# Swiglu of a hybrid layer: gate and up as seven block products in place of eight, u through memory, down as its own stage with eight sums side by side

## The chip, the core and the metric

The program runs on one core of one Trainium2 chip. The metric is the device time of one execution in microseconds; of the kernel before there are three runs. Everything is float32. The engines are named as the profile names them: PE (TensorE, the matrix products), PEld (its weight loads), DVE (VectorE), ACT (ScalarE), POOL (GpSimd) and SP (SyncE, which here only issues transfers). A tensor product is made three times, as high part by high part, high by low and low by high, of operands that are split into two float32r numbers.

## The reference, cut to what matters

```python
D_MODEL = 1024; SEQ = 2048; D_FF = 2816
def swiglu(h, w_gu, w_down):
    gate, up = jnp.split(h @ w_gu, 2, axis=-1)
    return (jax.nn.silu(gate) * up) @ w_down

def trunk_layer(x, ctx, mod_x, mod_c, lp, update_ctx):
    ...
    x = x + ga1 * branch_merge(px, fx, rwkv_output(yx, qx, lp), lp)
    hx2 = modulate(rmsnorm(x, lp["norm2_g"]), sh2, sc2)
    x = x + ga2 * swiglu(hx2, lp["w_gu"], lp["w_down"])
    ...
# and at the end: rmsnorm(x, final_norm_g)
```

The rest (input projection, a bidirectional scan, a Fourier branch) is computed by parts of the kernel that the change leaves as they are.

## The kernel before, in words

Data lie transposed: 128 channels on the partitions, tokens along the row. The 2048 tokens go in four blocks of 512 (`TB` gives their order 1, 2, 0, 3), and most tiles are 128x512 float32, 256 KB. Weights come as tiles of 128x128; `load_w` (lines 137 to 146) reads one column tile of a weight from memory in chunks of four rows of tiles (`wraw`, 256 KB each, two buffers), ACT copies the chunk into `whi` (L144, rounding to float32r) and DVE subtracts that for `wlo` (L145); `whi` and `wlo` have two buffers each. `mm3` (lines 148 to 153) then issues three products for each row of tiles: whi by high, whi by low, wlo by high (L151, L152, L153). `split` (L156 on ACT, L157 on DVE) does for activations what `load_w` does for weights. The program is written with tile pools; a scheduler sets the order of each engine's instructions at build time, and each engine then works through its own queue in that order, waiting on semaphores. A pool that is opened after another was closed in the same stretch of memory waits for the last user of that stretch.

Of the kernel's stages these matter here, with their times in the profiled execution:

- `gn_block` (lines 715 to 743), 16 blocks of 128 tokens that bring the scan's output into the layout of the next stage. The last three run between 1965 and 2006 us. Its tiles `gny`, `gnb`, `gnv` have six buffers; its result goes to memory (`o_dr`, L743, from POOL).
- `c_merge` (four token blocks, products named `pr`, 96 each) and `c_out` (products `po`, 192 each), in the order merge 0, merge 1, out 0, merge 2, out 1, merge 3, out 2, out 3. `c_merge` reads `o_dr` as `oraw`, and `gf` and `gr` from memory. `c_out` writes its rows `x1` to memory (`x1_dr`), sums squares (`acc`), and makes the row scale `rs` with a product named `rmsps` (L773), a square root on ACT and a reciprocal on DVE (L162). After out 0 the kernel also makes the SwiGLU's input for that token block at once (`h2_block`, L779 to L781, `XH0`).
- The SwiGLU from 2308 us, for two pairs of token blocks. `ff_in` makes the inputs `xh` and `xl` of a pair. For each of four groups of column tiles (6, 6, 5, 5 of 22), the gate product `pgt` and the up product `put` are made for both blocks of the pair with one load of the weight (24 products for each block and each tile), ACT and DVE make `tg = (tanh + 1) * gate * up` (L890, L891, L898), `split` makes `uh` and `ul`, and the group's part of the down product `pd` is added onto `x1f` in SBUF (L908). After the last group come squares, the sum over channels, the scale, the output (`oo`, L922) and its store.

PSUM has eight banks of 128x512: two in the pool `pmm`, six in `pcx`.

## Time and profile before

| what | us |
|---|---|
| runs: median of three (lowest, highest) | 3793.66 (3787.59, 3802.95) |
| the profiled execution: its span, first to last instruction | 3793.2 |
| PE busy, share of the span | 3527.7, 93% |
| DVE busy, share of the span | 2086.9, 55% |
| ACT busy, share of the span | 1397.3, 37% |
| mean clock granted to PE, of full speed | 0.954 |
| first `pr` product, first `po` product | 1980.1, 2044.1 |
| first `pgt` product, last `pd` product starts | 2308.4, 3767.8 |

The trace gives no time for the profiled execution other than its span, 0.5 us below the median of the runs. The page cuts the span into 40 slices of 95 us; the SwiGLU is the last 15 or so of them. In a row of a group, "busy" is the sum over its instructions, the number behind it the mean of one, and the last column is the time for which the engine stood idle just before them, with what ended it. Times of a product are latencies: products overlap, so their rate is read from counts over a window.

### The profile page before, as it was taken

How to read it: one execution, taken by the hardware profiler on the slowest of the kernel's cores; microseconds unless marked ns; L12 is line 12 of the kernel's file. 1: busy time of each engine (PE TensorE's matmuls, PEld its weight loads, DVE VectorE, ACT ScalarE, POOL GpSimd, SP SyncE). 2: the span in 40 equal slices, each digit the busy share in tenths (PEclk: the TensorE clock that was granted, in tenths of full speed). 3: DMA queues.
4: the chain of work that ended last, by engine and by line, in shares of the span. 5: the costliest groups of instructions: out<-in, count | busy, mean ns of one | idle time of the engine just before them, and what ended most of it. 6: DMA issues, size and time to landing. Idle time of an engine off the chain costs nothing.

```text
span 3793.2 us, 53448 instructions
## 1 busy us (share of the span) xinstructions
PE 3527.7 (93%) x20076; PEld 2885.6 (76%) x20076; DVE 2086.9 (55%) x4157; ACT 1397.3 (37%) x2618; POOL 490.4 (13%) x918
## 2 busy tenths in 40 slices
PE   5979899999999999998989798999999999999997
PEld 4858677677878878787777676888888878888886
DVE  7778776565676666667766664322233552232325
ACT  3776666533343444344443332212111321111122
POOL 0252333311121212121210000000000000000000
PEclk7989899999999999998989899999999999999999
DMA  6456544654454545557766554111111241111112
GB/s 221 138 188 200 165 157 171 212 164 124 139 164 137 154 137 166 166 147 234 214 205 227 167 192 144 46 55 42 53 44 53 88 141 44 54 46 49 50 49 69
DMA packets 282323, 494.75 MB, mean 130 GB/s; under 512 B 86576, under 2 KB 106032, under 8 KB 281552
## 3 DMA queue, kind: packets, MB, share of 16 engines
q1 hardware_dynamic: 241280, 363.74, 31.2%
q0 software_dynamic: 40784, 127.59, 10.1%
q8 instruction: 158, 2.59, 0.3%
q14 instruction: 101, 0.83, 0.1%
HBM read 371.00 MB, written 120.21 MB: 129 GB/s over the span
## 4 chain that ended last, share of the span: by engine, by line
PE 42%; issue 7%; DMA 2%; DVE 1%; ACT 1%; POOL 1%; SPq 0%; DVEq 0%; POOLq 0%; ACTq 0%
PE pd L152 4%; PE pd L153 4%; PE pd L151 4%; PE pgt L152 4%; PE pgt L151 4%; PE pgt L153 4%; PE put L153 4%; PE put L152 4%; PE put L151 4%; DMA gnb<-y_dr 1%; PE pf L152 0%; PE pf L151 0%; DMA gr<-g_dr 0%; PE pf L153 0%; POOL x_dr L822 0%
## 5 line engine op out<-in xcount | busy, mean ns | idle before, releaser
L144 ACT ACTIVATE whi<-wraw 128x512 fp32r<-128x512 f32 (+2 forms) x682 | 383.7, 600 | 1130.1 <-PE pd L152 338.7
L145 DVE TENSOR_TENSOR wlo<-wraw,whi 128x512 fp32r<-128x512 f32 (+2 forms) x682 | 427.9, 654 | 328.5 <-ACT whi L144 324.8
L151 PE MATMUL pgt<-xh,whi 128*128 128x512 f32 x704 | 276.6, 393 | 11.9 <-ACT xh L780 11.8
L151 PE MATMUL put<-xh,whi 128*128 128x512 f32 x704 | 275.3, 391 | 0.0
L152 PE MATMUL put<-xl,whi 128*128 128x512 f32 x704 | 275.0, 391 | 0.0
L153 PE MATMUL put<-xh,wlo 128*128 128x512 f32 x704 | 274.8, 390 | 0.0
L152 PE MATMUL pgt<-xl,whi 128*128 128x512 f32 x704 | 274.7, 390 | 0.1
L153 PE MATMUL pgt<-xh,wlo 128*128 128x512 f32 x704 | 274.6, 390 | 0.0
L152 PE MATMUL pd<-ul,whi 128*128 128x512 f32 x704 | 273.7, 389 | 0.0
L153 PE MATMUL pd<-uh,wlo 128*128 128x512 f32 x704 | 273.5, 389 | 0.0
L151 PE MATMUL pd<-uh,whi 128*128 128x512 f32 x704 | 273.2, 389 | 0.0
L151 PE MATMUL pxps<-hh,whi 128*128 128x512 f32 (+2 forms) x720 | 256.4, 357 | 17.6 <-ACT hh L198 6.3
L151 PE MATMUL fps<-fhh,whi 128*128 128x512 f32 x640 | 267.9, 419 | 3.8 <-ACT fhh L416 3.0
L152 PE MATMUL fps<-fhl,whi 128*128 128x512 f32 x640 | 259.7, 406 | 4.1 <-DVE fhl L417 4.1
L152 PE MATMUL pxps<-hl,whi 128*128 128x512 f32 (+2 forms) x720 | 254.5, 354 | 7.1 <-DVE hl L199 7.1
L153 PE MATMUL fps<-fhh,wlo 128*128 128x512 f32 x640 | 259.2, 405 | 0.0
L153 PE MATMUL pxps<-hh,wlo 128*128 128x512 f32 (+2 forms) x720 | 250.7, 350 | 0.2 <-DVE wlo L145 0.2
L908 DVE SCALAR_TENSOR_TENSOR x1f<-pd,ga2h,x1f 128x512 f32<-128x512 f32 x128 | 96.1, 751 | 279.1 <-PE pd L153 279.1
L898 DVE TENSOR_TENSOR tg<-tg,put 128x512 f32<-128x512 f32 x88 | 60.4, 687 | 261.0 <-PE put L153 260.9
L522 DVE TENSOR_TENSOR tm<-Q,AI 128x126 f32<-128x126 f32 (+22 forms) x558 | 141.1, 253 | 59.1 <-DMA AI<-ab_dr 34.6
L151 PEld LDWEIGHTS pxps<-hh,whi 128*128 128x128 f32 x720 | 141.6, 197 | 41.2 <-ACT hh L198 7.9
L151 PEld LDWEIGHTS pgt<-xh,whi 128*128 128x128 f32 x704 | 132.8, 189 | 41.5 <-ACT xh L780 13.0
(391 smaller groups left out, 7367.2 us busy)
## 6 DMA issues: line engine op xcount, KB each, us to landing
wraw<-w_in SPq DMA_DIRECT2D x250, 256.0 KB, 3.4
wraw<-w_gu SPq DMA_DIRECT2D x176, 256.0 KB, 3.0
ld<-zt_dr SPq DMA_DIRECT2D x36, 768.0 KB, 4.7
ld<-qr_dr SPq DMA_DIRECT2D x36, 512.0 KB, 6.3
wada<-w_ada SPq DMA_DIRECT2D x32, 512.0 KB, 4.6
g_dr<-fo POOLq DMA_DIRECT2D x64, 256.0 KB, 4.0
wraw<-w_out SPq DMA_DIRECT2D x64, 256.0 KB, 3.1
wraw<-w_down SPq DMA_DIRECT2D x64, 256.0 KB, 2.7
```

Source lines behind the costliest of these rows:

```text
L144: nc.scalar.activation(out=hi[:, k0:k1, :], in_=raw, func=AF.Copy)
L145: nc.vector.tensor_tensor(out=lo[:, k0:k1, :], in0=raw, in1=hi[:, k0:k1, :].bitcast(F32), op=ALU.subtract)
L151: nc.tensor.matmul(ps, wh[:, k, :], xh(k), start=start and k == 0, stop=False)
L152: nc.tensor.matmul(ps, wh[:, k, :], xl(k), start=False, stop=False)
L153: nc.tensor.matmul(ps, wl[:, k, :], xh(k), start=False, stop=stop and k == K - 1)
L522: nc.vector.tensor_tensor(out=tm[:, 0:M, 0:n], in0=Q[:, 0:M, j:j + 1].to_broadcast([128, M, n]), in1=AI[:, j, j + 1:32].unsqueeze(1).to_br ...
L898: nc.vector.tensor_tensor(out=tg, in0=tg, in1=pu, op=ALU.mult)
L908: nc.vector.scalar_tensor_tensor(out=x1[:, ct, :], in0=pd, scalar=ga2h[:, ct:ct + 1], in1=x1[:, ct, :], op0=ALU.mult, op1=ALU.add)
```

## The change

Gate and up for one column tile f of both and for both token blocks of a pair are seen as one product of 2x2 blocks: rows gate and up, inner halves (channels 0 to 511 and 512 to 1023, four tiles each), columns the two token blocks. It is made with seven block products (`B11`, `B21`, `T2`, `T3`, `T1`, `T4`, `B22`, twelve matrix products each) in place of eight, with sums of blocks before and after.

- The input side: the class `Operands` makes seven operands for a pair from `x1_dr`, split into high and low (`build(k)` for each of four tile indexes: four scalings on DVE, four biases on ACT, two differences on POOL, two on DVE, seven splits on ACT and DVE). For the first pair this lies inside the last `c_out`; `h2_block` and the pools around it go. For the second pair it lies inside the first `down`, with its reads issued from POOL.
- The weight side, in `up`: four chunks are read straight (`wA`, six buffers with `wS`), four sums or differences are made on DVE (`op`, L928), and seven operands are split into tiles with seven buffers (`hilo`).
- The result side, in `up`: one copy from PSUM on ACT (L956), seven additions on DVE (`add`, L941), two gates (L945 on ACT, L946 on DVE) and two products (L950 on DVE) whose results `u` go to memory (`u_dr`, from POOL). `B11` and `B21` use the two banks of `pmm`, the others the five of `pcx`; the eighth bank (`rm`) is for `rmsps`.
- `B11` and `B21` of the first three column tiles are made early, behind the last `c_out`.
- `down` is a stage of its own for each of the four token blocks: for each of 22 tiles f it reads a row of w_down (two chunks, through `load_w`) and u (one chunk, `ur`), splits them, and issues 24 products into eight sums that stay in eight banks; at the end they are added onto `x1` (L1024), squares and scale follow, and the output is stored (L1033, L1034). w_down is laid out by rows f on the host.
- The order is up of pair 0, down, down, up of pair 1, down, down.
- `c_merge` and `c_out` have the same work; their tiles lie in two pools (`ea` on the right side of SBUF, `eb` on the left, where the pool of `gn_block` was), with one buffer in each for `mh`, `ml` and `x1`, and eight buffers `t2` in `eb` in place of seven on the right side. `rs` of the last block is made inside `up`.

```diff
-    fa = ctx.enter_context(tc.tile_pool(name="fa", bufs=1))
-    pcx = ctx.enter_context(tc.tile_pool(name="pcx", bufs=6, space=PS))
+    u_dr = [D_([128, SEQ], f"u_dr{f}") for f in range(FT)]
...
+    pcx = fst.enter_context(tc.tile_pool(name="pcx", bufs=5, space=PS))
...
-        ps = pcx.tile([128, 512], F32, tag="cx", name="rmsps2")
+        ps = pcx.tile([128, 512], F32, tag="rm", name="rmsps2", bufs=1)
...
+    eb = eps.enter_context(tc.tile_pool(name="eb", bufs=1))
...
+    ea = eas.enter_context(tc.tile_pool(name="ea", bufs=1, side="right"))
...
+    def t2(name):
+        return eb.tile([128, 512], F32, tag="t2", name=name, bufs=8)
...
+    def out_stats(n, acc, rs):
+        sum_rs(acc, rs)
+        nc.gpsimd.dma_start(rs1_dr[TB[n]], rs[0:1, :])
+    OPS = ("B11", "B21", "T2", "T3", "T1", "T4", "B22")
+    class Operands:
+        def __init__(self, blk2, tmp, eng):
+            self.blk2, self.tmp, self.eng = blk2, tmp, eng
+            self.X = {o: [fh.tile([128, 4, 512], F32R, tag=f"{y}{o}", name=f"{y}{o}_{blk2}") for y in "hl"] for o in OPS}
...
+        def build(self, k):
+            b = {}
+            for m in range(2):
+                for hf in range(2):
+                    t0, kk = 512 * TB[2 * self.blk2 + hf], k + 4 * m
+                    x_ = b[m, hf] = self.tmp("x_")
+                    self.eng.dma_start(x_, x1_dr[:, kk, t0:t0 + 512])
+                    nc.vector.scalar_tensor_tensor(out=x_, in0=x_, scalar=gsc2[:, kk:kk + 1], in1=self.rs[hf], op0=ALU.mult, op1=ALU.mult)
+                    nc.scalar.activation(out=x_, in_=x_, func=AF.Identity, bias=mod[:, 24 + kk, 0:1])
+            b11, b12, b21, b22 = b[0, 0], b[0, 1], b[1, 0], b[1, 1]
+            t3 = self.tmp("t3")
+            def put_(o, x):
+                split(self.X[o][0][:, k, :], self.X[o][1][:, k, :], x)
+            def sub(o, x, y, eng=nc.gpsimd):
+                eng.tensor_tensor(out=o, in0=x, in1=y, op=ALU.subtract)
+            put_("B11", b11)
+            put_("B21", b21)
+            sub(t3, b22, b12)
+            sub(b12, b12, b11, nc.vector)
+            sub(b11, b22, b12, nc.vector)
+            put_("T2", b11)
+            put_("T3", t3)
+            put_("T1", b12)
+            sub(b21, b21, b11)
+            put_("T4", b21)
+            put_("B22", b22)
+    M = {}
+    M[0] = c_merge(0)
+    for n in range(3):
+        M[n + 1] = c_merge(n + 1)
+        acc = t2("acc")
+        c_out(n, M[n], acc)
+        out_stats(n, acc, t2("rs"))
+    eas.close()
+    fh = fst.enter_context(tc.tile_pool(name="fh", bufs=1, side="right"))
+    ops0 = Operands(0, t2, nc.sync)
+    acc3 = fh.tile([128, 512], F32, tag="rs", name="acc3", bufs=3)
+    c_out(3, M[3], acc3, lambda ct: ops0.build(ct // 2) if ct % 2 else None)
+    early = {}
+    for f in range(3):
+        w = load_w(I["w_gu"][f], KT)
+        early[f] = {}
+        for m, o in enumerate(OPS[:2]):
+            ps = pcx.tile([128, 512], F32, tag="cx", name="e" + o) if f < 2 else pmm.tile([128, 512], F32, tag="mm", name="e" + o)
+            mm3(ps, [x[:, 4 * m:4 * m + 4, :] for x in w], lambda k: ops0.X[o][0][:, k, :], lambda k: ops0.X[o][1][:, k, :], 4, 512)
+            early[f][o] = ps
+    eps.close()
+    ff = fst.enter_context(tc.tile_pool(name="ff", bufs=1))
+    def tmp(name):
+        return ff.tile([128, 512], F32, tag="t2", name=name, bufs=8)
+    def raw_(name):
+        return ff.tile([128, 512], F32, tag="raw", name=name, bufs=6)
+    def hilo(name):
+        return [ff.tile([128, 4, 128], F32R, tag=f"w{y}", name=f"{name}{y}", bufs=7) for y in "hl"]
+    def up(blk2, X, early, after=None):
+        TT = [512 * TB[2 * blk2 + hf] for hf in range(2)]
+        for f in range(FT):
+            if f == 1 and after:
+                after()
+            u2 = tmp("u2")
+            A = []
+            for src in (I["w_gu"][f], I["w_gu"][FT + f]):
+                for k0 in (0, 4):
+                    r = raw_("wA")
+                    nc.sync.dma_start(r.rearrange("p (k c) -> p k c", c=128), src[:, k0:k0 + 4, :])
+                    A.append(r)
+            a11, a12, a21, a22 = A
...
+            def prod(x, o):
+                if f in early and o in early[f]:
+                    return early[f][o]
+                ps = pmm.tile([128, 512], F32, tag="mm", name="p" + o) if o in OPS[:2] else pcx.tile([128, 512], F32, tag="cx", name="p" + o)
+                w = hilo("w" + o)
+                h_, l_ = [z.rearrange("p k c -> p (k c)") for z in w]
+                split(h_, l_, x)
+                mm3(ps, w, lambda k: X[o][0][:, k, :], lambda k: X[o][1][:, k, :], 4, 512)
+                return ps
...
+            def gate(c):
+                g_ = tmp("tg")
+                nc.scalar.activation(out=g_, in_=c, func=AF.Tanh, scale=0.5)
+                nc.vector.scalar_tensor_tensor(out=g_, in0=g_, scalar=1.0, in1=c, op0=ALU.add, op1=ALU.mult)
+                return g_
+            def u_out(hf, c, g_):
+                nc.vector.tensor_tensor(out=c, in0=c, in1=g_, op=ALU.mult)
+                nc.gpsimd.dma_start(u_dr[f][:, TT[hf]:TT[hf] + 512], c)
+            s1 = raw_("wS")
+            op(s1, a21, a22, ALU.add)
+            p = prod(a11, "B11")
+            nc.scalar.activation(out=u2, in_=p, func=AF.Copy)
+            op(a21, a11, a21, ALU.subtract)
+            op(a11, s1, a11, ALU.subtract)
+            p = prod(a12, "B21")
+            c11 = tmp("c11")
+            add(c11, u2, p)
+            op(a12, a12, a11, ALU.subtract)
+            p = prod(a11, "T2")
+            add(u2, u2, p)
+            g0 = gate(c11)
+            p = prod(a21, "T3")
+            u3 = tmp("u3")
+            add(u3, u2, p)
+            p = prod(s1, "T1")
+            add(u2, u2, p)
+            c22 = tmp("c22")
+            add(c22, u3, p)
+            p = prod(a22, "T4")
+            add(u3, u3, p)
+            u_out(0, u3, g0)
+            p = prod(a12, "B22")
+            add(u2, u2, p)
+            u_out(1, c22, gate(u2))
+    def down(tb, between=None):
+        t0 = 512 * tb
+        def bank(ct):
+            if ct == 7:
+                return pcx.tile([128, 512], F32, tag="rm", name="pd7", bufs=1)
+            return (pcx if ct < 5 else pmm).tile([128, 512], F32, tag="cx" if ct < 5 else "mm", name=f"pd{ct}")
+        PD = [bank(ct) for ct in range(7)]
+        OPN = {}
+        def load(f):
+            w = load_w(I["w_down"][f], KT)
+            r = ff.tile([128, 512], F32, tag="ur", name="u_", bufs=2)
+            nc.sync.dma_start(r, u_dr[f][:, t0:t0 + 512])
+            u = hilo("u")
+            h_, l_ = [z.rearrange("p k c -> p (k c)") for z in u]
+            split(h_, l_, r)
+            return w, h_, l_
+        def mm(f, ct):
+            (wh, wl), uh, ul = OPN[f]
+            for i, (x, y) in enumerate(((wh, uh), (wh, ul), (wl, uh))):
+                nc.tensor.matmul(PD[ct], x[:, ct, :], y, start=f == 0 and i == 0, stop=f == FT - 1 and i == 2)
+        for f in range(2):
+            OPN[f] = load(f)
+            for ct in range(7):
+                mm(f, ct)
+        PD.append(bank(7))
+        for f in range(2):
+            mm(f, 7)
+        for f in range(2, FT):
+            OPN[f] = load(f)
+            for ct in range(8):
+                mm(f, ct)
+            if between:
+                between(f)
+        X1 = []
+        acc = fh.tile([128, 512], F32, tag="rs", name=f"accf{tb}", bufs=3)
+        for ct in range(8):
+            x1 = tmp("x1f")
+            X1.append(x1)
+            nc.sync.dma_start(x1, x1_dr[:, ct, t0:t0 + 512])
+            nc.vector.scalar_tensor_tensor(out=x1, in0=PD[ct], scalar=ga2h[:, ct:ct + 1], in1=x1, op0=ALU.mult, op1=ALU.add)
...
+    up(0, ops0.X, early, lambda: out_stats(3, acc3, fh.tile([128, 512], F32, tag="rs", name="rs3", bufs=3)))
+    ops1 = Operands(1, raw_, nc.gpsimd)
+    down(TB[0], lambda f: ops1.build(f // 4 - 1) if f % 4 == 0 and 4 <= f < 20 else None)
+    down(TB[1])
+    up(1, ops1.X, {})
+    down(TB[2])
+    down(TB[3])
...
-        "w_gu": tiles(a["w_gu"][0]), "w_down": tiles(a["w_down"][0]),
+        "w_gu": tiles(a["w_gu"][0]), "w_down": np.ascontiguousarray(a["w_down"][0].reshape(FT, 128, KT, 128)),
```

Three places show how the instructions move. The first is SP's queue between the last blocks of `gn_block` (L716 to L720) and merge 0. Before:

```order
L718 DMA gnv_18497<-bv_dr_69 128x512
L797 DMA oraw_18587<-o_dr_95 128x512
L797 DMA oraw_18591<-o_dr_95 128x512
L797 DMA oraw_18595<-o_dr_95 128x512
L716 DMA gny_18531<-y_dr0_93 128x512
L797 DMA oraw_18599<-o_dr_95 128x512
L801 DMA gf_18603<-fm_dr0_98 128x512
L803 DMA gr_18605<-g_dr8_80 128x512
L720 DMA sg_18537<-sg_dr_70 128x128
L717 DMA gnb_18532<-y_dr1_94 128x512
```

In the changed kernel, from the same read of `gnv` on (`x1_1` is the row tile of out 0, 2 MB):

```order
L718 DMA gnv_18497<-bv_dr_69 128x512
L819 DMA x1_1_19076<-xT 128x8x512
L716 DMA gny_18531<-y_dr0_93 128x512
L720 DMA sg_18537<-sg_dr_70 128x128
L717 DMA gnb_18532<-y_dr1_94 128x512
L718 DMA gnv_18533<-bv_dr_69 128x512
L800 DMA oraw_18607<-o_dr_95 128x512
L800 DMA oraw_18611<-o_dr_95 128x512
L800 DMA oraw_18615<-o_dr_95 128x512
L800 DMA oraw_18619<-o_dr_95 128x512
```

The reads of merge 0 stood among those of the last `gn_block`; now they stand behind all of them, and the row tile of out 0 stands ahead of the last block's reads.

The second place is DVE's queue in the last `c_out`. Before, one column tile is an addition onto `x`, two `wlo` and an addition of squares, and after the last one `rmsps` and the reciprocal follow, and then the input of the SwiGLU's second block:

```order
L821 SCALAR_TENSOR_TENSOR x_3_20543<-po,ga1h,x_3_20543 128x512
L145 TENSOR_TENSOR wlo<-wraw,whi 128x512 x2
L826 TENSOR_TENSOR acc<-acc,sqk 128x512
L160 TENSOR_SCALAR rs<-rmsps_20865 128x512
L162 RECIPROCAL rs<-rs 128x512
L779 SCALAR_TENSOR_TENSOR a__20879<-x__20880,gsc_263,rs_20877 128x512
L781 SCALAR_TENSOR_TENSOR xl_1_20876<-a__20879,mod,xh_1_20875 128x512
```

In the changed kernel (`hB`, `lB`, `hT`, `lT` are the high and low parts of the operands):

```order
L145 TENSOR_TENSOR wlo<-wraw,whi 128x512 x2
L829 TENSOR_TENSOR acc_20553<-acc_20553,sqk 128x512
L857 SCALAR_TENSOR_TENSOR x__20634<-x__20634,gsc_263,rs_0_0_20549 128x512
L857 SCALAR_TENSOR_TENSOR x__20638<-x__20638,gsc_263,rs_0_1_20551 128x512
L857 SCALAR_TENSOR_TENSOR x__20642<-x__20642,gsc_263,rs_0_0_20549 128x512
L824 SCALAR_TENSOR_TENSOR x_3_20554<-po,ga1h,x_3_20554 128x512
L157 TENSOR_TENSOR lB_0_20536<-x__20634,hB_0_20535 128x512
L857 SCALAR_TENSOR_TENSOR x__20646<-x__20646,gsc_263,rs_0_1_20551 128x512
L157 TENSOR_TENSOR lB_0_20538<-x__20642,hB_0_20537 128x512
```

Between the additions onto `x` there now stand scalings and low parts of the operands. From the first addition of this `c_out` to the last low part, DVE's queue holds 24 scalings or additions onto `x`, 62 other operations on 128x512 and two reciprocals.

The third place is where a pair of token blocks ends and the next begins. Before, on DVE (two blocks finish together; `pgt` and `put` are the next pair's first products):

```order
L160 TENSOR_SCALAR rsf_1_25535<-rmsps_25536 128x512
L922 SCALAR_TENSOR_TENSOR oo<-x1f_0_20927,vec,rsf_0_25505 128x512 x8
L162 RECIPROCAL rsf_1_25535<-rsf_1_25535 128x512
L145 TENSOR_TENSOR wlo<-wraw,whi 128x512
L922 SCALAR_TENSOR_TENSOR oo<-x1f_1_20929,vec,rsf_1_25535 128x512 x8
L891 SCALAR_TENSOR_TENSOR tg<-tg,pgt 128x512 x2
L898 TENSOR_TENSOR tg<-tg,put 128x512 x2
```

In the changed kernel, on DVE, from the second `down` to the second `up` (`c`, `u` are the sums after the products, `pB`, `pT` the products):

```order
L160 TENSOR_SCALAR rsf_26469<-rmsps_26470 128x512
L157 TENSOR_TENSOR wB22l<-wA,wB22h 128x512
L162 RECIPROCAL rsf_26469<-rsf_26469 128x512
L1033 SCALAR_TENSOR_TENSOR x1f<-x1f,vec,rsf_26469 128x512 x8
L941 TENSOR_TENSOR c_26539<-u_26491,pB_26522 128x512
L941 TENSOR_TENSOR u_26491<-u_26491,pT_26542 128x512
L946 SCALAR_TENSOR_TENSOR tg<-tg,c_26539 128x512
```

and on PE at the same place, within the last of the seven products of the first column tile (`pB_26656` is `B11` of the second column tile):

```order
L151 MATMUL pB_26622<-hB_1_24431,wB22h 128x512
L780 MATMUL rmsps_26470<-accf_26422,cn 128x512
L152 MATMUL pB_26622<-lB_1_24432,wB22h 128x512
L153 MATMUL pB_26622<-hB_1_24431,wB22l 128x512
L151 MATMUL pB_26656<-hB_1_24419,wB11h 128x512
```

On PE `rmsps` stands behind 79 products of the new pair, and on DVE the first sum that frees a bank of the new pair stands behind the scale and the eight outputs of the old block.

199 lines of the change are left out of this document (62 added, 137 removed).

## The prediction

> **What bounds the kernel now.** I read the page first: busy times, slices and the chain.
>
> ```profile
> PE 3527.7 (93%) x20076; PEld 2885.6 (76%) x20076; DVE 2086.9 (55%) x4157; ACT 1397.3 (37%) x2618; POOL 490.4 (13%) x918
> PE   5979899999999999998989798999999999999997
> DVE  7778776565676666667766664322233552232325
> PE 42%; issue 7%; DMA 2%; DVE 1%; ACT 1%; POOL 1%; SPq 0%; DVEq 0%; POOLq 0%; ACTq 0%
> ```
>
> PE is the longest, and in the SwiGLU (last 16 slices) it is full but for the last, with DVE at two to five tenths. Next the windows: length, then busy time and count on PE, PEld, DVE, ACT and POOL, then granted clock, DMA share and GB/s.
>
> ```profile
> 2400.00:3000.00 600.00, 600.00 (x2649) 496.99 (x2648) 188.66 (x301) 112.58 (x208) 0.00 (x0) 1.00 0.17 52
> 3000.00:3100.00 100.00, 97.62 (x427) 79.68 (x426) 69.42 (x104) 35.13 (x61) 0.00 (x0) 1.00 0.47 152
> ```
>
> 600 us hold 2649 products at full clock, one per 0.2265 us, with no gap. There only fewer products shorten anything. The second window has the boundary of the pairs, the one stop inside.
>
> **Part 1, the products.** For a pair and a column tile f, gate and up were 2 x 2 x 24 = 96 products; now 7 x 12 = 84. Over 22 tiles and two pairs 528 go: 528 x 0.2265 = **-119.6 us**, if PE stays dense. Whether DVE lets it, these groups tell (busy, mean ns | idle before):
>
> ```profile
> L157 DVE TENSOR_TENSOR ul<-tg,uh 128x512 fp32r<-128x512 f32 x88 | 60.5, 688 | 28.7 <-ACT uh L156 28.6
> L898 DVE TENSOR_TENSOR tg<-tg,put 128x512 f32<-128x512 f32 x88 | 60.4, 687 | 261.0 <-PE put L153 260.9
> L891 DVE SCALAR_TENSOR_TENSOR tg<-tg,pgt 128x512 f32<-128x512 f32 x88 | 60.1, 684 | 156.1 <-ACT tg L890 156.1
> L156 ACT ACTIVATE uh<-tg 128x512 fp32r<-128x512 f32 x88 | 55.0, 625 | 193.3 <-DVE tg L898 193.1
> 2187.97 2.43 DVE L157 TENSOR_TENSOR ol<-oraw,oh 128x512 fp32r<-128x512 f32 x4
> ```
>
> In `up` DVE has 22 operations for each f: 7 low parts, 4 operand sums, 7 additions, 2 gates, 2 products. At 0.687 alone that is 15.1 us, at the 0.61 of the last row (four in 2.43, back to back) 13.4. PE needs 84 x 0.2265 = 19.03. ACT has 10, at 0.625 6.3 us. A weight buffer of `hilo` frees one f before it is needed again, and a bank (seven for seven products) likewise, so a wait up to several us is covered; I take PE as the bound. What could hide here is a gap behind each DVE operation; that is a rival below.
>
> **Part 2, merge 0.** Its reads now wait for `gn_block`'s pool, whose last transfer goes out here:
>
> ```profile
> 1980.00:2044.00 64.00, 54.25 (x216) 41.18 (x217) 47.77 (x81) 25.26 (x48) 2.15 (x3) 0.90 0.89 301
> 2005.85 0.71 POOL L743 DMA_DIRECT2D o_dr<-gnb  x1 [11.88 <-DMA gr<-g_dr]
> gf<-fm_dr SPq DMA_DIRECT2D x32, 256.0 KB, 4.6
> ```
>
> Before, the two merges run from 1980 to 2044 us with DMA 0.89 busy: 192 products need 43.5 of the 64. Now they start about 2006 + 4.6 (a landing) = 2010.6, and dense they end at 2054: +10; if the reads run early there is no loss, if DMA stays the limit behind the late start it is twice that. I take **+9** (0 to +18).
>
> **Part 3, out 0 to merge 2.** `h2_block` goes (16 DVE operations and a reciprocal between out 0 and merge 2). PE's waits at the start of merge 2 and of merge 3, which has no such block ahead:
>
> ```profile
> 2105.55 0.79 PE L151 MATMUL pr<-oh,whi 128*128 128x512 f32 x1 [14.19 <-ACT oh L156]
> 2123.28 0.79 PE L151 MATMUL pr<-oh,whi 128*128 128x512 f32 x1 [4.49 <-ACT whi L144]
> 2186.08 1.22 PE L151 MATMUL pr<-oh,whi 128*128 128x512 f32 x2 [2.81 <-ACT oh L156]
> 2188.65 0.80 PE L152 MATMUL pr<-ol,whi 128*128 128x512 f32 x1 [1.35 <-DVE ol L157]
> ```
>
> Merge 2 becomes like merge 3: 18.68 - 4.16 = **-14.5 us**. The splits of `oraw` then come last, as there.
>
> **Part 4, the last `c_out` and the SwiGLU's start.**
>
> ```profile
> 2260.60:2304.70 44.10, 44.08 (x194) 35.99 (x192) 21.49 (x29) 12.58 (x23) 4.31 (x8) 1.00 0.41 136
> 2304.70:2346.00 41.30, 26.84 (x88) 20.36 (x89) 17.16 (x21) 8.65 (x13) 1.05 (x2) 0.79 0.55 188
> 2322.86 0.80 PE L151 MATMUL pgt<-xh,whi 128*128 128x512 f32 x1 [7.44 <-ACT xh L780]
> 2323.45 0.63 PE L151 MATMUL put<-xh,whi 128*128 128x512 f32 x1
> 2327.62 0.39 PE L152 MATMUL put<-xl,whi 128*128 128x512 f32 x1
> 2327.85 0.39 PE L153 MATMUL put<-xh,wlo 128*128 128x512 f32 x1
> PE rmsps L773 <- DVE acc L826: 2.6, 1, 2.6
> 3771.70 3.35 DVE L162 RECIPROCAL rsf<-rsf 128x512 f32<-128x512 f32 x1 [1.25 <-ACT rsf L161]
> 3784.19 5.39 DVE L922 SCALAR_TENSOR_TENSOR oo<-x1f,vec,rsf 128x512 f32<-128x512 f32 x8
> ```
>
> `c_out` 3 fills 44.1 us, and in the next 41.3 PE makes 88 products, two of them `rmsps`: 85.4 - 86 x 0.2265 = 65.9 us until a dense SwiGLU would have begun. Now the operands of pair 0 are made inside, and DVE's queue holds 24 scalings (0.67, eight in 5.39), 62 others (0.61) and two reciprocals (3.35): 60.6 us, longer than PE's 43.5. The queue's start waits for the first sum, 24 products or 5.4 us: 66; its last part waits for the reads of the last `x1`, a landing and four short operations, about 6.5: 72.5. PE meanwhile makes 72 early products, 16.3 us ahead: 56. DVE gives PE the operands tile by tile, and some early products wait too; for those hand-offs I leave 4. So 60 for 66: **-6** (-13 to +5). POOL's eight differences stand beside this; the nearest row on that engine is a fill of the same size, and above it stands DVE's reciprocal, 0.53 to 3.35 each:
>
> ```profile
> L516 POOL MEMSET Q<- 128x512 f32 x18 | 9.5, 526 | 37.7 <-DMA tb_dr<-Q 37.7
> ```
>
> DVE then has other tiles to work on; uncovered, two in the last tile would cost 1 to 7 us, inside the bound. At out 2 to out 3, `rmsps` (2.6 us wait) goes behind other products: **-2**.
>
> **Part 5, the seams.** `up` and `down` alternate with new sums, so there are five seams where before there was one. The last `pd` product of the kernel, the one seam, and the kernel's end:
>
> ```profile
> 3767.82 0.40 PE L153 MATMUL pd<-uh,wlo 128*128 128x512 f32 x1
> 3048.85 1.13 PE L773 MATMUL rmsps<-acc,cn 128*128 128x512 f32 x2 [2.38 <-DVE acc L913]
> 3768.00:3794.00 26.00, 2.20 (x5) 0.50 (x4) 19.93 (x22) 3.17 (x4) 0.00 (x0) 0.63 0.46 161
> ```
>
> The seam cost 2.4 + 1.1 = 3.5, which goes: **-3.5**. Up to down: all banks but two are free; the last additions, 2 each, two times: **+4**. Down to down: the new block's first products wait for the eight additions onto `x1` (0.7 each, PE needs one bank after the other) and `rmsps` (1.1); and on DVE the reciprocal (3.35) and the outputs (5.4) stand ahead of some `wlo`, where two f of products (10 us) cover: **+6** each (2 to 12), twice, **+12**. Down to up (once): PE has the 79 products of the third order place, 17.9 us, plus `rmsps` 1.1, and then needs a bank that DVE frees behind additions, root (0.6), reciprocal (3.35) and outputs (5.4), at about 8 x 0.7 + 7 x 0.7 + 1.1 + 0.7 + 0.6 + 3.35 + 5.4 + 0.7 = 22 to 30 us from the end of the block, so 5 to 8 us idle. After the idle time of 7.44 the first eleven products took 4.76 us (2322.86 to 2327.62) instead of 2.49, 2.3 us more, and from there they stand 0.23 apart; after the 2.38 the window shows full clock. **+10** (4 to 15). The Trainium skill, "TensorE: Matmul & The Clock Gate", "The HAM clock gate", puts the point at an idle window of about 3.4 us, which both rows agree with; by it the two down-to-down seams would add up to 4.6 if they idle so long. Sum of seams **+26** (14 to 45), and **-3.5**.
>
> **Part 6, `down` itself.** 22 x 24 x 0.2265 = 119.7 us for a block, as many products as before. Per f: 5.44 us of PE, three low parts on DVE (2.1), three copies on ACT (1.9), 768 KB by
>
> ```profile
> wraw<-w_out SPq DMA_DIRECT2D x64, 256.0 KB, 3.1
> wraw<-w_down SPq DMA_DIRECT2D x64, 256.0 KB, 2.7
> ```
>
> or 145 GB/s. The `c_out` window has the same two chunks through the same two buffers for 24 products, at 136 GB/s, and 194 products in 44.1 us, dense. So nothing is added; the 44 writes of `u` from POOL and the operands of pair 1 (four times 13 DVE operations, 9 us in four f, 22 us) lie beside it.
>
> **Part 7, the end.** After the last product 25.1 us remain (3767.8 + 0.4 to 3793.2), with two reciprocals and twice eight outputs. Now one block ends: eight additions and squares (6), `rmsps`, root, reciprocal, eight outputs, a landing: 20: **-5** (-9 to 0).
>
> **The sum.** -119.6 + 9 - 14.5 - 6 - 2 - 3.5 + 26 - 5 = -115.6. The profiled execution's 3793.2 becomes 3677.6; the median of the runs stands 0.5 above its span: **3678**.
>
> **The rivals.** *DVE paces `up`.* 22 operations with seven hand-offs exposed, each as long as an operation (0.69): 15.1 + 4.8 = 20.0 per f, 1 above PE's, x 44 = +43: 3721. For it: a sum waits for ACT and PE in turn. Against: one f of buffers. *Every seam costs as the worst stops here* (14.19 + 4.49 = 18.7): 5 x 18.7 = 94 for 26, with end and start as above, some +84 for hand-offs of operands too: 3762. *`down` starves, slower than before*: a chunk's buffer comes free only behind its low part, two buffers, three chunks. A buffer's round is a landing, a copy (0.63) and a low part (0.69): 4.4 us at 3.1. If landings take 4.6, as `gf`'s, and the low part stands behind two other DVE operations, it is 7.3 per f instead of 5.44: 88 x 1.86 = +164: 3842. It decides from (3793.7 - 3678) / 88 = 1.31 more per f, 6.75 us. Against it stands the dense `c_out`. *DVE empties behind each operation, slower too*: with gaps of half an operation to a whole one (0.34 to 0.69) 22 of them take 22.6 to 30.3 us per f, 3.6 to 11.3 above PE's, x 44 = +158 to +497: 3836 to 4175; it decides from a gap of 0.30. The four operations in 2.43 and eight in 5.39, without such gaps, nearly exclude it. The Trainium skill, "VectorE: DVE Perf Modes", "The DRAIN you can't avoid", states such a gap, of about the duration less 266 ns (0.42, by which the kernel would take 3913). That the products do not fall is excluded by the order, which has them.
>
> **How the numbers follow.** Forecast 0.71 (3646 to 3722, with all unknown costs at their lower ends, -12 - 9 - 7 - 4 = -32, or their upper, 19 + 9 + 11 + 5 = +44); DVE 0.10; seams 0.07; starving in full 0.04, near break-even 0.02; DVE emptying 0.02; better than 3645, by seams that cost nothing, 0.04. The range reaches over the forecast and the DVE case, to 3740: 0.19 is left out. 0.5% (19 us, about what a measurement can tell) bounds the chances: faster 0.71 + 0.10 + 0.07 + 0.04 = 0.92, same 0.02, slower 0.04 + 0.02 = 0.06 (starving near break-even counts as the same).
>
> **What would show it.** Right: in a 400 us window of `up` and of `down` PE full, 4.41 products per us, DVE at 0.7 to 0.8 in `up`; first `po` near 2053; seams of 2 to 10 us; about 20 us behind the last product. Wrong: PE waits for low parts or additions inside `up` (DVE case), for `wraw` copies or `u` inside `down` (starving), seams near 20, or an `up` group on DVE with gaps of 0.3 or more behind each operation.

## The result, and the profile after

The changed kernel takes 3702.55 us (median of four runs, 3702.01 to 3713.41) against 3794.4 for the kernel before (four runs, 3787.59 to 3802.95): a ratio of 0.9766, 95% interval 0.9744 to 0.9787. It is faster by 91.9 us, where 116 were forecast; 3702.55 lies in the range of 3645 to 3740, 24.6 above the forecast value. The profiled execution has a span of 3700.3 us, 92.9 less than before, and the account below is made against that.

From the page of the changed kernel: busy times, the slices of PE and DVE, the chain.

```profile
PE 3424.6 (93%) x19548; PEld 2796.1 (76%) x19548; DVE 2495.4 (67%) x4765; ACT 1595.9 (43%) x2898; POOL 579.3 (16%) x1038
PE   5989889999999999999996999899999999999997
DVE  7777776566676675668776667877785477777344
PE 23%; issue 9%; DVE 2%; DMA 1%; POOL 1%; ACT 0%; SPq 0%; DVEq 0%; POOLq 0%; ACTq 0%
```

PE has the 528 products less (20076 to 19548), DVE 409 us more. DVE is now at 0.7 to 0.8 where `up` runs, and PE's slices are full there all the same. The windows, one in the first `up`, one in the first `down`, one in the last but one:

```profile
2400.00:2700.00 300.00, 300.00 (x1325) 248.43 (x1324) 222.98 (x347) 96.95 (x157) 16.80 (x31) 1.00 0.26 84
2760.00:2860.00 100.00, 100.00 (x443) 82.81 (x442) 53.81 (x82) 43.45 (x76) 9.14 (x8) 1.00 0.54 172
3440.00:3550.00 110.00, 110.00 (x487) 91.12 (x486) 45.07 (x71) 37.70 (x66) 0.00 (x0) 1.00 0.45 147
```

1325 products in 300 us are 4.42 per us, as before. So the two long stages are dense, as forecast, and all of the difference lies between them. PE's waits there, from the timeline (start, duration, what waited, how long and for what):

```profile
2334.82 0.79 PE L151 MATMUL pT<-hT,wT2h 128*128 128x512 f32 x1 [9.56 <-ACT wT2h L156]
2751.36 0.50 PE L1003 MATMUL pd<-uh,whi 128*128 128x512 f32 x1 [1.02 <-ACT whi L144]
2759.11 0.50 PE L1003 MATMUL pd<-uh,whi 128*128 128x512 f32 x1 [2.02 <-ACT whi L144]
2895.34 0.80 PE L1003 MATMUL pd<-uh,whi 128*128 128x512 f32 x1 [6.98 <-ACT whi L144]
3023.65 0.80 PE L151 MATMUL pB<-hB,wB11h 128*128 128x512 f32 x1 [8.72 <-ACT u L956]
3577.74 0.80 PE L1003 MATMUL pd<-uh,whi 128*128 128x512 f32 x1 [6.47 <-ACT whi L144]
3684.14 2.07 PE L780 MATMUL rmsps<-accf,cn 128*128 128x512 f32 x2 [5.74 <-DVE accf L1029]
```

They are the start of the first `up`, the third row of w_down after the first and third `down` (2895, 3577), the second column tile of the second `up` (3023), and the end. Behind each of the long ones a product takes 0.80 in place of 0.39: PE starts again at the slow clock.

For the account by stages the scan's last product (`pz`) is a good mark, since the code ahead of it is the same in both kernels. Before, then after:

```profile
L594 PE MATMUL pz<-UV,BT x1152: 222/222/370, 825.6 to 1971.5; 128*64 128x64 f32 x192
```

```profile
L594 PE MATMUL pz<-UV,BT x1152: 222/222/369, 827.1 to 1963.7; 128*64 128x64 f32 x192
L151 PE MATMUL pr<-oh,whi x128: 387/389/796, 1995.0 to 2205.1; 128*128 128x512 f32 x128
L151 PE MATMUL po<-mh,whi x256: 389/389/397, 2047.6 to 2294.2; 128*128 128x512 f32 x128
```

| stage | before | after | difference | forecast |
|---|---|---|---|---|
| start to the scan's last product | 1971.5 | 1963.7 | -7.8 | 0 |
| to the first `po` | 72.6 | 83.9 | +11.3 | +9 |
| to the start of out 3 (2260.6, 2249.3) | 216.5 | 201.7 | -14.8 | -16.5 |
| to where a dense SwiGLU would begin | 65.9 | 71.0 | +5.1 | -6 |
| the products of the SwiGLU at 0.2265 | 1435.1 | 1315.5 | -119.6 | -119.6 |
| its waits up to the last product | 6.6 | 42.6 | +36.0 | +22.5 |
| the rest to the end | 25.0 | 21.9 | -3.1 | -5 |
| sum | 3793.2 | 3700.3 | -92.9 | -115.6 |

Out 3 starts with the first of the last 192 `po` products. The fourth line is made as in the prediction: from there to 2345 us are 95.7 us with 109 products of the SwiGLU, 95.7 - 24.7. The first line is not counted as the change's: the profiled executions of the experiments, with the same code ahead of that mark, have it between 1957 and 1974 us. So of the 92.9 us some 85 belong to the change in this pair of executions, and 23 to 31 us of the forecast gain (counted with and without that line) did not come: 11 at the first `up`'s start and 13 in the seams, for the most part.

### The profile page after: what moved, and what is told of

Its sections match the earlier page's. It is cut to its first block, busy times and chain, and to the rows that moved or that the text cites. A ratio compares the mean times of both kernels' runs of the same rounds, so it can differ in the third digit from the quotient of the medians.

```text
span 3700.3 us, 54802 instructions
## 1 busy us (share of the span) xinstructions
PE 3424.6 (93%) x19548; PEld 2796.1 (76%) x19548; DVE 2495.4 (67%) x4765; ACT 1595.9 (43%) x2898; POOL 579.3 (16%) x1038
## 3 DMA queue, kind: packets, MB, share of 16 engines
q8 instruction: 155, 2.54, 0.3%
## 5 line engine op out<-in xcount | busy, mean ns | idle before, releaser
L144 ACT ACTIVATE whi<-wraw 128x512 fp32r<-128x512 f32 x560 | 333.2, 626 | 704.3 <-PE pd L1003 196.0
L145 DVE TENSOR_TENSOR wlo<-wraw,whi 128x512 fp32r<-128x512 f32 x560 | 374.4, 688 | 369.7 <-ACT whi L144 356.2
L941 DVE TENSOR_TENSOR u<-u,pT 128x512 f32<-128x512 f32 x176 | 120.8, 686 | 142.6 <-PE pT L153 140.8
L1003 PEld LDWEIGHTS pd<-uh,whi 128*128 128x128 f32 x704 | 133.2, 189 | 53.2 <-ACT whi L144 22.5
L152 PEld LDWEIGHTS pxps<-hl,whi 128*128 128x128 f32 x720 | 142.1, 197 | 29.0 <-DVE hl L199 8.7
L153 PEld LDWEIGHTS pxps<-hh,wlo 128*128 128x128 f32 x720 | 141.6, 197 | 21.3 <-issue 4.8
L1003 PEld LDWEIGHTS pd<-ul,whi 128*128 128x128 f32 x704 | 133.4, 189 | 27.6
L1003 PEld LDWEIGHTS pd<-uh,wlo 128*128 128x128 f32 x704 | 132.1, 188 | 28.7 <-DVE wlo L145 1.4
L152 PEld LDWEIGHTS fps<-fhl,whi 128*128 128x128 f32 x640 | 123.4, 193 | 35.5 <-issue 5.4
L524 DVE TENSOR_TENSOR Q<-Q,tm 128x126 f32<-128x126 f32 (+22 forms) x558 | 140.7, 252 | 13.6
```

The source lines that it names most:

```text
L144: nc.scalar.activation(out=hi[:, k0:k1, :], in_=raw, func=AF.Copy)
L145: nc.vector.tensor_tensor(out=lo[:, k0:k1, :], in0=raw, in1=hi[:, k0:k1, :].bitcast(F32), op=ALU.subtract)
L152: nc.tensor.matmul(ps, wh[:, k, :], xl(k), start=False, stop=False)
L153: nc.tensor.matmul(ps, wl[:, k, :], xh(k), start=False, stop=stop and k == K - 1)
L524: nc.vector.tensor_tensor(out=Q[:, 0:M, j + 1:32], in0=Q[:, 0:M, j + 1:32], in1=tm[:, 0:M, 0:n], op=ALU.subtract)
L941: nc.vector.tensor_tensor(out=o, in0=x, in1=y, op=ALU.add)
```

## The experiments

Each is one edit of the changed kernel unless it says otherwise. Since the stages ahead of the merges vary, time is also counted from the first `po` product to the end: 1652.7 us in the changed kernel (3700.3 - 2047.6). That figure has a spread of its own: e11, which alters nothing behind the first `po`, has 1647.4, so the changed kernel's trace is the slower of the two that can be compared over the whole stretch. Differences under about 5 us are therefore believed only where the waits of the trace show them.

| run | median, us (lowest, highest) | ratio to before, interval | first `po` to end |
|---|---|---|---|
| e1_twelve_more | 3827.35 (3821.73, 3829.66) | 1.0089 (1.0071, 1.0108) | 1774.2 |
| e2_low_twice | 3708.85 (3693.29, 3710.27) | 0.9781 (0.9751, 0.9811) | 1659.3 |
| e3_rs_pool | 3703.86 (3697.29, 3714.55) | 0.9771 (0.9749, 0.9794) | 1649.8 |
| e4_outs_pool | 3711.94 (3707.91, 3714.1) | 0.9789 (0.9774, 0.9804) | 1656.0 |
| e5_own_u2 | 3696.05 (3690.63, 3702.89) | 0.9749 (0.973, 0.9768) | 1645.6 |
| e7_no_early | 3709.92 (3707.51, 3717.22) | 0.9775 (0.9751, 0.9799) | 1663.9 |
| e8_subs_dve | 3692.11 (3684.43, 3696.35) | 0.9746 (0.9715, 0.9777) | 1647.9 |
| e9_x1_late | 3700.0 (3694.69, 3705.76) | 0.9767 (0.974, 0.9794) | 1651.4 |
| e10_all | 3693.14 (3689.81, 3693.85) | 0.9747 (0.9724, 0.977) | 1630.5 |
| e11_merge0_right | 3690.41 (3683.24, 3692.12) | 0.9722 (0.9701, 0.9744) | 1647.4 |
| e12_best | 3669.13 (3663.5, 3679.52) | 0.9673 (0.9647, 0.9699) | 1632.6 |

### Do the products set the pace?

```diff
-            def prod(x, o):
+            def prod(x, o, times=1):
...
-                mm3(ps, w, lambda k: X[o][0][:, k, :], lambda k: X[o][1][:, k, :], 4, 512)
+                for _ in range(times):
+                    mm3(ps, w, lambda k: X[o][0][:, k, :], lambda k: X[o][1][:, k, :], 4, 512)
...
-            p = prod(a12, "B22")
+            p = prod(a12, "B22", 2)
```

> The last block product of every column tile (B22) is made twice, the second time over the first, so that PE has 96 products for a pair and a column tile as before the change; everything else of the changed kernel stays. Products set the pace of up: 528 x 0.2265 = +119.6 us on the changed kernel's 3702.6, 3822. Rival, DVE or the hand-offs set the pace of up: part of the added products lies in waits that are there anyway, under +80, 3780 or less. By the first, 3822 against 3794 before is also the price of all the rest of the change, +28.

Measured from the first `po`: 1774.2 - 1652.7 = +121.5 us. The 528 products cost what the rate says (119.6), within the spread, and no large part of them was hidden. The other half of the answer is the ratio to before, 1.0089: with the products given back, the rest of the change costs 35 us (3827.35 against 3792.17 in the same comparison). The prediction's other terms add up to +4. That is where it was off. The next edit makes the low part of each weight operand twice:

```diff
                 split(h_, l_, x)
+                nc.vector.tensor_tensor(out=l_, in0=x, in1=h_.bitcast(F32), op=ALU.subtract)
```

> In up the low part of each of the seven weight operands is made twice, with the same result, so that DVE has 29 operations for a column tile in place of 22. In the changed kernel's up 347 DVE operations took 222.98 us of 300, 0.643 each. Theory, PE sets the pace and DVE's operations follow each other without gaps: 29 x 0.643 = 18.6 us, just under PE's 19.03, PE stays full, 0 to +6 us. Rival, DVE sets the pace as soon as the sum of its operations with their hand-offs comes near: 29 x 0.687 = 19.9 and more, +39 us or over.

The windows of the first and the second `up` with 29 DVE operations for each column tile:

```profile
2400.00:2700.00 300.00, 300.00 (x1325) 248.41 (x1324) 285.87 (x469) 94.78 (x158) 16.72 (x31) 1.00 0.27 87
3100.00:3400.00 300.00, 300.00 (x1326) 248.39 (x1325) 282.50 (x458) 97.43 (x159) 17.25 (x32) 1.00 0.25 83
```

DVE is 0.95 busy, with 0.61 us per operation (285.87 / 469), and PE still makes 1325 products. The +6.6 us lie at the seams. The wait at 3029, behind the second `up`'s first tile, is 10.40 us, where DVE now has more to work off; the one at 3585 is 8.48, but `down` isn't altered, and other runs have 6.19 to 7.37 there, so that part may be spread. DVE's pace was no near danger: seven more operations for each tile fitted.

### The seams between blocks

What DVE, SP and ACT do ahead of the wait of 6.98 us, and PE and DMA in windows of 5 us around it, in the changed kernel:

```profile
2880.22 5.38 DVE L1033 SCALAR_TENSOR_TENSOR x1f<-x1f,vec,rsf 128x512 f32<-128x512 f32 x8
2885.52 1.28 DVE L145 TENSOR_TENSOR wlo<-wraw,whi 128x512 fp32r<-128x512 f32 x2
2885.57 0.33 SPq L1023 DMA_DIRECT2D x1f<-x_dr  x1
2885.99 0.85 SPq L1034 DMA_DIRECT2D out_T<-x1f  x2
2887.42 1.37 SPq L1034 DMA_DIRECT2D out_T<-x1f  x2
2888.89 0.43 SPq L143 DMA_DIRECT2D wraw<-w_down  x1
2891.43 3.32 SPq L1023 DMA_DIRECT2D x1f<-x_dr  x4
2894.66 0.63 ACT L144 ACTIVATE whi<-wraw 128x512 fp32r<-128x512 f32 x1 [5.63 <-DMA wraw<-w_down]
```

```profile
2875.00:2880.00 5.00, 5.00 (x23) 3.99 (x22) 5.00 (x5) 1.92 (x4) 0.00 (x0) 1.00 0.09 12
2880.00:2885.00 5.00, 4.21 (x19) 3.15 (x18) 5.00 (x9) 1.90 (x3) 0.00 (x0) 1.00 0.92 305
2890.00:2895.00 5.00, 0.00 (x0) 0.00 (x0) 0.00 (x0) 0.34 (x1) 0.00 (x0) 0.66 0.97 331
```

The chunk of w_down goes out at 2888.89, behind stores of the old block (which wait for DVE's outputs) and reads of `x1` for the end of the next block (which wait for the stores' buffers), and ACT can copy it 5.8 us later where the median landing is 2.9, with DMA 0.97 busy. Either could be the cause. There is a third candidate: the chunk goes into one of two buffers, which is free when a low part on DVE (2885.52) has read it, and that low part stands behind the eight outputs. First SP's queue:

```diff
-            nc.sync.dma_start(x1, x1_dr[:, ct, t0:t0 + 512])
+            nc.gpsimd.dma_start(x1, x1_dr[:, ct, t0:t0 + 512])
...
-            nc.sync.dma_start(out_T[128 * k:128 * k + 128, t0:t0 + 512], X1[k])
+            nc.gpsimd.dma_start(out_T[128 * k:128 * k + 128, t0:t0 + 512], X1[k])
```

> The reads of x1 and the stores of the output in down go out from POOL and no longer from SP. Theory, SP's queue: at the end of a block the stores wait for DVE's eight outputs and the reads of the next x1 for the buffers that the stores free, and the chunks of w_down stand behind them; the two waits of 6.98 and 6.47 us go, and the slow clock behind each (2.3), -16 to -18 us, 3685. Rival, DVE's queue (the reciprocal and eight outputs ahead of the low parts): the waits stay at 4 or more each, at most -6, 3697.

```profile
2901.94 0.80 PE L1003 MATMUL pd<-uh,whi 128*128 128x512 f32 x1 [4.02 <-ACT whi L144]
3581.84 0.50 PE L1003 MATMUL pd<-uh,whi 128*128 128x512 f32 x1 [1.54 <-ACT whi L144]
3592.19 0.80 PE L1003 MATMUL pd<-uh,whi 128*128 128x512 f32 x1 [4.60 <-ACT whi L144]
```

6.98 became 4.02, 6.47 became 1.54 + 4.60, and in all nothing was gained (1656.0): a miss. SP is free, but the same 4 MB go out at the same moment, and a later chunk is late. Then the crowd, with the stores left on SP:

```diff
+        X1 = []
...
+            if f == 14:
+                for ct in range(8):
+                    x1 = tmp("x1f")
+                    X1.append(x1)
+                    nc.gpsimd.tensor_copy(x1[:, 0:1], OPN[f][1][:, 0:1].bitcast(F32))
+                    nc.sync.dma_start(x1, x1_dr[:, ct, t0:t0 + 512])
...
-        X1 = []
...
-            x1 = tmp("x1f")
-            X1.append(x1)
-            nc.sync.dma_start(x1, x1_dr[:, ct, t0:t0 + 512])
+            x1 = X1[ct]
```

> The reads of x1 in down are held back until the 15th of the 22 rows (each waits for a copy of one column on POOL, written over by the read); the stores stay on SP. Theory, the transfers crowd: at the end of a block 2 MB of stores and 2 MB of reads for the next block's end go out in 20 us with DMA 0.92 to 1.04 busy, and the chunks of w_down among them land late; without the reads the two waits of 6.98 and 6.47 us fall below 3 and the slow clock goes, -8 to -14 us from the first po product to the end. Rival, the chunks are late because they stand behind the stores on SP, which wait for DVE's outputs: the waits stay above 5, 0 to -2.

```profile
2802.42 0.50 PE L1004 MATMUL pd<-uh,whi 128*128 128x512 f32 x1 [2.08 <-ACT whi L144]
2891.55 0.50 PE L1004 MATMUL pd<-uh,whi 128*128 128x512 f32 x1 [3.41 <-ACT whi L144]
3569.92 0.79 PE L1004 MATMUL pd<-uh,whi 128*128 128x512 f32 x1 [3.90 <-ACT whi L144]
```

The waits halve, to 3.41 and 3.90, but 2.08 us come back where the reads now go out, in the middle of a block; 1651.4 is no gain that the spread lets one claim. Neither edit is enough alone; with both (below) the two waits are 2.84 and 1.85 in e10, 3.87 and 1.25 in e12.

For the first of the two waits, the traces give the time from the start of the low part that frees the buffer to the chunk's issue on SP, and from there to the start of ACT's copy:

| trace | low part to issue | issue to copy | PE's wait |
|---|---|---|---|
| changed kernel | 3.37 | 5.77 | 6.98 |
| e4, SP free of stores and `x1` | 0.71 | 5.47 | 4.02 |
| e9, `x1` read later | 1.03 | 4.54 | 3.41 |
| e10, both and three more edits | 0.71 | 4.30 | 2.84 |
| e12, as e10 and merge 0 | 0.71 | 5.32 | 3.87 |

In each row the wait is the sum of the two times less 2.16 or 2.17. So both causes are real: SP's queue took 2.7 us here, and the slow landing some 2.9 against the median. With 0.71 and 2.9 the wait would still be 1.4 (an estimate from these rows), because the low part stands behind DVE's outputs: by this estimate DVE's queue, the prediction's reason, is the smallest of the three. No edit brought the landing down to its median.

The seam from the second `down` to the second `up`, 8.72 us:

```diff
-            u2 = tmp("u2")
+            u2 = ff.tile([128, 512], F32, tag="sq", name="u2", bufs=2)
...
-            c11 = tmp("c11")
+            c11 = ff.tile([128, 512], F32, tag="ur", name="c11", bufs=2)
```

> In up the sums u2 and c11 get buffers that are idle there (those of the squares and of down's u) in place of t2 buffers, all eight of which hold x1f of the block that ends. Theory, buffers: the wait of 8.72 us at the second up is for a buffer of x1f, and goes with the slow clock behind it, -9 to -11 us, 3692. Rival, DVE's queue: the reciprocal and the eight outputs stand ahead of the sums and of the next low parts all the same, and PE then waits one block product later, 0 to -3 us, 3701.

```profile
3017.03 0.58 ACT L956 ACTIVATE u<-pB 128x512 f32<-128x512 f32 x1
3018.85 5.38 DVE L1033 SCALAR_TENSOR_TENSOR x1f<-x1f,vec,rsf 128x512 f32<-128x512 f32 x8
3025.58 0.47 PE L151 MATMUL pB<-hB,wB21h 128*128 128x512 f32 x1 [0.74 <-ACT wT2h L156]
```

The copy out of the bank no longer waits for DVE's eight outputs, PE goes on through them, and of 8.72 us 0.74 are left; in all it is 7.1 us less than in the changed kernel's trace. It was a buffer, held by `x1f` until its store had landed. The rival, that DVE's queue makes PE wait all the same, is out for this seam.

### The start of the first `up`

```diff
-                nc.sync.dma_start(rs, rs1_dr[TB[2 * blk2 + hf]].to_broadcast([128, 512]))
+                eng.dma_start(rs, rs1_dr[TB[2 * blk2 + hf]].to_broadcast([128, 512]))
```

> The two reads of the row scale for the second pair's operands (L847) go out from POOL and no longer from SP. Theory, SP's queue: one of these reads waits for the scale of the last block, and the first weight chunks of up stand behind it, so PE waits 9.6 us for the first T2; with the reads gone from SP the wait falls below 3 us and the slow clock behind it goes, -8 to -12 us, 3692. Rival, DVE is late anyway with the operands and w_down's first chunks still stand ahead of the weights: the wait stays at 6 or more, at most -3, 3700.

```profile
2317.17 0.68 DVE L157 TENSOR_TENSOR lT<-x__20987,hT 128x512 fp32r<-128x512 f32 x1
2317.93 1.76 SPq L923 DMA_DIRECT2D wA<-w_gu  x4
2327.48 0.79 PE L151 MATMUL pT<-hT,wT2h 128*128 128x512 f32 x1 [7.42 <-ACT wT2h L156]
```

And the same wait in e11 (below):

```profile
2326.20 0.80 PE L151 MATMUL pT<-hT,wT2h 128*128 128x512 f32 x1 [6.89 <-ACT wT2h L156]
```

9.56 became 7.42: a miss of the theory. e11 alters nothing here and has 6.89, so even these 2 us are not shown to come from the edit. SP was free in time, but the weights still go out only when DVE ends the last low part of the operands (2317.85): their tiles lie where the operands' tiles lay, and that pool frees with its last reader. In the traces of all eleven experiments and of the changed kernel that read follows the end of the last low part by 0.07 to 0.11 us. The queue was not the cause, the pool and DVE ahead of it were. In the changed kernel the same place reads:

```profile
2319.71 1.66 POOL L866 TENSOR_TENSOR x__20987<-x__20987,x__20979 128x512 f32<-128x512 f32 x1 [2.58 <-DVE x__20979 L866]
2320.15 1.77 DVE L157 TENSOR_TENSOR lT<-x__20983,hT 128x512 fp32r<-128x512 f32 x1
2323.97 0.68 DVE L157 TENSOR_TENSOR lT<-x__20987,hT 128x512 fp32r<-128x512 f32 x1
2324.76 1.75 SPq L923 DMA_DIRECT2D wA<-w_gu  x4
2331.48 0.69 DVE L928 TENSOR_TENSOR wS<-wA 128x512 f32<-128x512 f32 x1 [2.93 <-DMA wA<-w_gu]
```

The last low part ends at 2324.65, 75.4 us after out 3's start where the forecast had 72.5, and from there to the product are 10.2 us, for which it had no term. A DVE operation beside a POOL operation takes 1.77 in place of 0.68; seven operations in this stage (not eight, as the expectation below counts) are so stretched, by 5.4 us in all. The next edit tests what that costs:

```diff
-            def sub(o, x, y, eng=nc.gpsimd):
+            def sub(o, x, y, eng=nc.vector):
```

> The differences of the operands that POOL makes (two for each tile index) go to DVE; the sums stay the same. Theory, POOL's help is not free: in the last c_out eight DVE operations beside POOL's differences took 1.1 to 1.8 us in place of 0.68 to 0.74, some 5.4 us in all, as much as eight more DVE operations (8 x 0.68 = 5.4), and the last tile's difference takes 1.66 us on POOL: 0 to -3 us, counted from the first po product (1652.7 us in the changed kernel) to the end. Rival, POOL's help is free: +5.

```profile
2310.96 0.69 DVE L157 TENSOR_TENSOR lT<-x__20987,hT 128x512 fp32r<-128x512 f32 x1
```

The same low part now stands 271.5 us behind the first `po` (2310.96 - 2039.5) and stood 276.4 (2323.97 - 2047.6): 4.9 sooner, although DVE has eight operations more. But the changed kernel's trace is at the late end here: the eight traces in which neither the differences nor the early products are altered (the changed kernel, e1 to e5, e9, e11) have 272.2 to 276.4. The three with the differences on DVE (e8, e10, e12) have 271.4 to 271.7, ahead of all of these. So the gain is about 1 to 5 us, and the rival's +5 is out: POOL's help cost at least what it saved. The total, 1647.9, can't be told from e11's 1647.4. How much the early products cover:

```diff
-    for f in range(3):
+    for f in range(0):
```

> The 72 early products (B11 and B21 of the first three column tiles) are not made ahead but in up, from split weights as those of the other column tiles. Theory, they are work for PE while DVE finishes the operands: without them PE waits from the last c_out on until the weights have come behind the operands, +13 to +16 us from the first po product to the end (72 x 0.2265 = 16.3 at most). Rival, the weights loaded for them delay the operands on DVE and the reads: 0 to +6.

```profile
2322.64 0.69 DVE L157 TENSOR_TENSOR lT<-x__20987,hT 128x512 fp32r<-128x512 f32 x1
2327.05 0.79 PE L151 MATMUL pB<-hB,wB11h 128*128 128x512 f32 x1 [18.75 <-DMA wA<-w_gu]
2320.00:2345.00 25.00, 17.95 (x70) 14.68 (x71) 19.66 (x30) 10.46 (x17) 1.64 (x1) 0.77 0.39 126
```

The whole is 11.2 us longer, between theory and rival, but the stage itself says less: by 2345 us 70 products of the SwiGLU are made, so a dense one would have begun at 2345 - 70 x 0.2265 = 2329.1, 277.9 behind the first `po`; in the changed kernel it is 2320.3 - 2047.6 = 272.7, and in the other seven of those eight traces 268.5 to 273.0. The early products are worth 5 to 9 us here, less than the 16.3 us of PE that they fill; the rest of the 11.2 lies at later seams, in waits that vary from run to run (1.24 and 0.37 us more behind the first block's). Two things eat the difference. Their weights hold the operands up on DVE by 1 to 5 us (last low part 271.4 behind the first `po`, 272.2 to 276.4 with them). And without them PE starts with `B11`, which needs one chunk, 3.7 us behind the operands, where `T2` needs the last of four chunks and three operations, 10.2.

### The start of the merges

```diff
+        def t2m(name):
+            return ea.tile([128, 512], F32, tag="t2a", name=name, bufs=7) if n == 0 else t2(name)
...
-            raw = t2("oraw")
+            raw = t2m("oraw")
```

and so for `gf` and `gr`.

> The tiles oraw, gf and gr of merge 0 alone lie in the pool on the right side of SBUF (seven buffers), so that they don't wait for the pool of the last layout blocks; everything else of the changed kernel stays. Theory, that wait costs 11 us: from the start of the scan's last product (pz) to the first po product are 83.9 us in the changed kernel and 72.6 before; it falls to 72 to 75, -9 to -12. Rival, transfers bound that stage wherever the reads start (DMA 0.89 busy there): the reads only come earlier, 0 to -4.

```profile
L594 PE MATMUL pz<-UV,BT x1152: 221/222/369, 827.7 to 1966.6; 128*64 128x64 f32 x192
L151 PE MATMUL po<-mh,whi x256: 387/389/397, 2042.9 to 2288.1; 128*128 128x512 f32 x128
```

2042.9 - 1966.6 = 76.3 us, against 83.9: 7.6 of the 11.3 come back, a little less than expected, and well past the rival (the changed kernel and the other nine experiments that leave merge 0 alone have 82.6 to 84.7). The remaining 3.7 are not explained. The ratio falls to 0.9722.

### Together

> Together: own buffers for u2 and c11, reads of the row scale from POOL, reads of x1 held back, the stores of the output from POOL, differences on DVE. If the gains add (7 for the buffers, as measured from the first po product; 3 for the scale, as measured; 12 for the reads with the stores off SP; 0 to 3 for the differences): -22 to -25, 1628 to 1631 from the first po product to the end, some 3678 in all. If the waits change places, half of that or less: 1640 or more.

```profile
2898.01 0.50 PE L1004 MATMUL pd<-uh,whi 128*128 128x512 f32 x1 [2.84 <-ACT whi L144]
3027.84 0.47 PE L151 MATMUL pB<-hB,wB21h 128*128 128x512 f32 x1 [0.73 <-ACT wT2h L156]
3564.37 0.50 PE L1004 MATMUL pd<-uh,whi 128*128 128x512 f32 x1 [1.85 <-ACT whi L144]
```

1630.5 from the first `po` product, -22.2, as expected of gains that add; against e11's 1647.4 it is -16.9, and the 3 us expected for the row scale were not shown above, so only the sum is confirmed. The whole is 3693.14 and not 3678: in the profiled execution the stages ahead of the merges were among the slow ones (first `po` at 2057.5).

> The five edits that were tried together, and merge 0 on the right side. If both add: 1630.5 us from the first po product to the end as with the five, and 72 to 75 from the scan's last product to the first po product, 3682 in all (3693 - 11), a ratio of 0.972 to before. If the start of the merges takes nothing off: 3693, 0.975.

```profile
L594 PE MATMUL pz<-UV,BT x1152: 221/222/369, 825.4 to 1962.6; 128*64 128x64 f32 x192
L151 PE MATMUL po<-mh,whi x256: 389/389/397, 2037.9 to 2281.1; 128*128 128x512 f32 x128
```

1632.6 from the first `po`, 75.3 from the scan's last product to it, and 3669.13 us in all, less than the 3682 expected: in the profiled execution the stages ahead were early this time (first `po` at 2037.9). Its ratio of 0.9673 (0.9647 to 0.9699) is clear of the changed kernel's 0.9766 (0.9744 to 0.9787): this version beats both kernels.

## Why the prediction held, and where it was off

- **The products** (-119.6): right, to 2 us (e1, with a spread of some 5), and PE as the bound of `up`: right, with seven DVE operations for each tile to spare (e2). The rivals on DVE's pace, and the one with a gap behind each operation, are out. `down` was dense too, at 172 and 147 GB/s, so its starving did not come; it was not pushed further to find the point where it would.
- **Merge 0** (+9): right in mechanism, and near in size: +11.3, of which e11 gave 7.6 back.
- **Out 0 to merge 2, and out 2 to out 3** (-16.5): -14.8, right. Merge 2 now waits 2.39 and 1.77 us at its start (at 2097 and 2100), 4.16 as forecast; a wait of 2.02 at 2110 is new.
- **The first `up`'s start** (-6, at most +5): the sign was wrong, +5.1. The step that failed is that PE goes on as soon as DVE has made the operands, "72.5" after out 3's start: the sum has no term for the weights of the first `T2`, and these came 10.2 us behind the operands, because their pool was free only when the last low part was done. DVE itself ended at 75.4, not 72.5: it was busy for 66.8 us where the sum had "60.6", of which 5.4 are the stretch beside POOL's differences, which have no term in the sum; the others were sized well (the trace has 64 of the short ones, not 62). The "6.5" for the reads of the last `x1` was too much, DVE waited 3.0 in all. So 2.9 and 10.2 more, and 1.9 for the slow clock (the first nine products took 3.93 us, at 0.2265 they need 2.04), less the 4 that were left for hand-offs, give the 11 between 60 and 71.0.
- **The seams** (+26, less the old one's 3.5): the mechanism was half right and the size off. "Up to down" 4: 3.0. "Down to up" 10: 8.7 and the slow clock, about 10, but the cause named was a bank behind DVE's queue; it was a buffer behind the stores (e5). "Down to down, +6 each": the waits over a seam add to 8.9 (0.78, 0.79, 0.38, 6.98) and 9.0 (0.78, 0.96, 0.23, 6.47, 0.57), plus `rmsps` and the slow clock, some 12 each, the upper end of its "2 to 12". The step took DVE's queue and forgot SP's: chunks of w_down behind stores and reads, and those 4 MB in flight with them (e4, e9, e10). With the first `up`'s start it is the largest miss.
- **The end** (-5): -3.1; 5.74 us go until the squares are summed.
- Two small slips of the sum, 119.7 for 119.6 (`down`) and 25.1 for 25.0 (the end), change nothing.

So the forecast was too low because costs where stages meet were counted on the engines and not on what the next stage's loads wait for: a pool, a queue, and the memory traffic beside them. By the two traces 22.7 us are missing, and 30.5 without the 7.8 ahead of the merges: 11.1 at the first `up`'s start, 13.5 in the waits, 2.3, 1.7 and 1.9 in the other lines. That the traces show 22.7 and not 30.5 is luck; the range would have held either.

## What to carry to other kernels

In this kernel a saving in products was worth its rate while PE was full, so the work of a forecast lay at the places where stages meet. There, list for each queue that issues transfers what stands ahead of the next stage's first load, what those entries wait for (a store for its result, a prefetch for a buffer that the store frees), when the load's own buffer or pool comes free, and how many bytes leave at that moment; two such causes can stand in one wait, so that removing either alone shows little in the total. And read a gain against more than one trace of the same code: several here are no larger than the spread. Give a tile that the next stage needs at once a buffer that the old stage's stores don't hold.
